# SwiGLU with seven products of quarters for eight, and the sums of weights made by adding transfers

## The chip, the cores and the metric

The kernel runs on one core of one Trainium2 chip. The metric is the device time of one execution in microseconds (us). All weights lie in HBM as float32 and are read once in the kernel before.

## The reference

A trunk of two layers over 256 tokens of 1024 features. Each layer is a SwiGLU, a mixer (attention) and a second SwiGLU, so there are four SwiGLU blocks, and only these are changed:

```python
D_MODEL, SEQ, DEPTH, D_FF = 1024, 256, 2, 2816

def rms_norm(x, g):
    y = x * lax.rsqrt(jnp.mean(x * x, axis=-1, keepdims=True) + EPS)
    return y * g

def swiglu(h, w_gate, w_up, w_down):
    return (jax.nn.silu(h @ w_gate) * (h @ w_up)) @ w_down

for layer in range(DEPTH):
    x = x + 0.5 * swiglu(rms_norm(x, ffn1_norm[layer]), *ffn1[layer])
    x = x + mixer(rms_norm(x, mix_norm[layer]))      # even or odd
    x = x + 0.5 * swiglu(rms_norm(x, ffn2_norm[layer]), *ffn2[layer])
return rms_norm(x, final_norm)
```

`w_gate` and `w_up` are 1024 x 2816, `w_down` is 2816 x 1024.

## The kernel before

**Matmuls of split numbers.** Every factor of a large product is split into a high part and a low part (`high_part`, a ScalarE copy that rounds to float32r, L319; `low_part`, a VectorE subtraction, L322). A product is three matmuls: high by high (L311), high by low (L312), low by high (L313), all in `mm`. A *piece* is one 128-row slice of weights, 512 or 384 columns wide; splitting a piece is one ScalarE and one VectorE instruction. The activations stand still (128 x 128 tiles, loaded with LDWEIGHTS) and the weights stream past them. The 256 tokens are two tiles of 128 (`tt`), so each split piece of a SwiGLU is used twice, in six matmuls.

**A SwiGLU block** (`ffn`). Gate and up go through the columns in chunks, `FF_CHUNKS = [512, 512, 512, 512, 384, 384]`. For each chunk the eight row slices of the gate are multiplied for both token tiles into PSUM tiles `s`, then those of up into `pj`. `silu` (L500, ScalarE) and `glu` (L505, VectorE) follow, then `split_T` turns the result with four TensorE transposes (L394) and splits it. The RMS factor `rstd` of a token is applied there, in `silu` and `glu`; only the gain is in the turned and split input `hT` (`prepare`, L366 to L356). The down product then runs over 22 row slices into four banks, tags `o`, `pj`, `s`, `s`. PSUM has eight banks: two `pj`, three `s`, one `o`, two `tp`.

**What sets the order.** The order on TensorE, ScalarE, VectorE and SyncE is the order in which the program emits; GpSimd's is planned by the framework. Work beside the matmuls is written as generators. `tick` runs once after each three matmuls: it steps them, and adds `rate` (0.53 pieces) to a budget from which `supply` splits the next piece, while fewer than `AHEAD = 14` split pieces wait. So the splits run up to 14 pieces ahead of the matmuls. `plan` lists the units of weights (four row slices, 1 MiB at 512 columns) in the order of their use; `load` fetches one when the first piece of the unit before is split, by one transfer from SyncE's queue (L268) into one of three `raw` buffers.

Of the kernel before, what the change touches and what calls it, by code (L numbers as in the profile page):

```python
# [1 line left out]

# [14 lines left out]
P = 128  # L17
# [22 lines left out]
X_WAIT = 5  # L40
R_WAIT = 3
GLU_WAIT = 5
NAT_WAIT = 2
ROPE_WAIT = 3
# [22 lines left out]


class Piece:


    def __init__(self, raw, uses, first):
        self.raw, self.uses, self.first, self.parts = raw, uses, first, None

# [48 lines left out]
class Trunk:  # L123
# [4 lines left out]
    def __init__(self, ctx, tc, a, out):  # L128
        self.ctx, self.tc, self.nc, self.a, self.out = ctx, tc, tc.nc, a, out
        pool = lambda name, bufs, **kw: ctx.enter_context(tc.tile_pool(name=name, bufs=bufs, **kw))  # L130
        self.one = pool("one", 1)
        self.ph = None
        self.raw = pool("raw", 3)
        self.wp = pool("wp", PIECES)
# [6 lines left out]
        self.units, self.whole, self.queue, self.live, self.due, self.half = self.plan(), [], [], 0, 0, None  # L141

    def name(self, s):
# [43 lines left out]
    def tick(self, supply=True):  # L187
        self.low()
        for task in list(self.tasks):
            task[0] -= 1  # L190
            if task[0] <= 0 and task[1] is not None:
                self.step(task)
        if supply:
            self.due += self.rate
            if self.due >= 1 and self.live < AHEAD:
                self.due = min(self.due - 1, 1)
                self.supply()


    def plan(self):  # L200


        a = self.a

        def columns(w2d, spans, units=None):
            w = sum(n for _, n in spans)
            k = 0
            for nk in units or (4, 4):
                pieces, o = [], 0
                for c0, n in spans:  # L210
                    src = w2d[k * P : (k + nk) * P, c0 : c0 + n].rearrange("(k p) n -> p k n", p=P)
                    pieces.append(((slice(0, P), slice(0, nk), slice(o, o + n)), src))
                    o += n
                yield pieces, nk, w, [2]
                k += nk

        def ffn(n, l, stage):
            c0 = 0
            for w in FF_CHUNKS:
                first = FIRST if stage == 0 and c0 == 0 else None  # L220
                yield from columns(a[n + "_w_gate"][l], [(c0, w)], first)
                yield from columns(a[n + "_w_up"][l], [(c0, w)])
                c0 += w
            for f in range(0, FF // P, 2):
                src = a[n + "_w_down"][l][f * P : (f + 2) * P, :].rearrange("(k p) n -> p k n", p=P)
                yield [(slice(0, P), src)], 2, D, [2, 3 if stage == 5 else 2]

        def even():
            w_in, w_out = a["even_w_in"][0], a["even_w_out"][0]
            for spans in ([(512, 256), (1280, 256)], [(768, 512)], [(0, 512)]):  # L230
                yield from columns(w_in, spans)
            for g in (1, 0):
                for nh in range(2):
                    pieces = []
                    for s in range(2):
                        r0 = g * 512 + s * 256
                        src = w_out[r0 : r0 + 256, nh * 512 : nh * 512 + 512].rearrange("(j p) n -> p j n", p=HD)
                        pieces.append((slice(64 * s, 64 * s + 64), src))
                    yield pieces, 4, 512, [2]

        def odd():
            w_qkv, w_out = a["odd_w_qkv"][0], a["odd_w_out"][0]
            for g in range(2):
                for i in (1, 0, 2):
                    yield from columns(w_qkv, [(i * D + g * 512, 512)])
            for g in range(2):
                for nh in range(2):
                    src = w_out[g * 512 : g * 512 + 512, nh * 512 : nh * 512 + 512].rearrange("(j p) n -> p j n", p=P)
                    yield [(slice(0, P), src)], 4, 512, [2]

# [7 lines left out]
    def load(self):  # L258
        unit = next(self.units, None)
        if unit is None:  # L260
            return
        pieces, nk, w, uses = unit
        if nk * w > 512:
            raw = self.raw.tile([P, nk, w], F32, tag="raw", name=self.name("raw"))
        else:
            raw = self.t([P, nk, w], "raw", 2)
        for sl, src in pieces:
            self.nc.sync.dma_start(raw[sl], src)  # L268
        new = [
            Piece(raw[:, k, c : min(c + 512, w)], uses[c // 512], k + c == 0) for k in range(nk) for c in range(0, w, 512)  # L270
        ]
        self.whole += new
        self.queue += new

    def supply(self):

        self.low()
        if not self.whole:
            return
        piece = self.whole.pop(0)  # L280
        if piece.first:
            self.load()
        w = piece.raw.shape[-1]
        hi = self.wp.tile([P, w], F32R, tag="hi", name=self.name("hi"))
        lo = self.wp.tile([P, w], F32R, tag="lo", name=self.name("lo"))
        self.high_part(hi, piece.raw)
        piece.parts = (hi, lo)
        self.half = piece
        self.live += 1

    def low(self):

        if self.half is not None:
            self.low_part(self.half.parts[1], self.half.raw, self.half.parts[0])
            self.half = None

# [6 lines left out]

    def mm(self, ps, lh, piece, first, last, sl=slice(None)):
        while piece.parts is None:
            self.supply()
        if piece is self.half:
            self.low()
        (h, l), (wh, wl) = lh, (t[:, sl] for t in piece.parts)
        mm = self.nc.tensor.matmul  # L310
        mm(ps, h, wh, start=first, stop=False)  # L311
# [33 lines left out]

    def part_h(self, tb, tt, i, k, j):

        hi = self.one.tile([P, P], F32R, tag=f"hT{tt}{k}h", name=self.name("th"))
        lo = self.one.tile([P, P], F32R, tag=f"hT{tt}{k}l", name=self.name("tl"))
        gain = self.gains[:, i * KD + k : i * KD + k + 1]  # L350
# [9 lines left out]
    def prepare(self, tt, i, half, dest):  # L360
# [6 lines left out]
        yield 1  # L367
        his = [self.part_h(tb, tt, i, half * 4 + j, j) for j in range(4)]
        yield 1
# [65 lines left out]
    def project(self, hT, pieces, tag):  # L435
        ps = self.bank(tag)
        n = len(pieces)
        for k in range(n):
            self.mm(ps[:, : pieces[k].raw.shape[-1]], hT[k], pieces[k], k == 0, k == n - 1)
        return ps  # L440
# [12 lines left out]
    def first_gates(self, W):  # L453
# [5 lines left out]
        def turn(j):  # L459
# [6 lines left out]
            return banks  # L466

        def parts(j, banks):
            for tt in range(NT):
                now.hT[tt] += [self.part_h(banks[tt], tt, 0, 2 * j + i, i) for i in range(2)]  # L470
            for i in range(2):
# [11 lines left out]
        for j in range(KD // 2):  # L483
# [3 lines left out]
            for k in (2 * j, 2 * j + 1):  # L487
                for tt in range(NT):
                    self.mm(ps[tt], now.hT[tt][k], W[k], k == 0, k == KD - 1)
        return ps  # L490

    def ffn(self):
        nc = self.nc
        self.rate = RATE
        gT = [[], []]
        tasks = [[], []]

        def silu(tt, w, g, s):
            yield 1
            nc.scalar.activation(s[:, :w], g[:, :w], AF.Silu, scale=self.rstd_of(tt))  # L500

        def glu(tt, ci, w, u, s):
            yield 1
            m = self.t([P, 512], "glu", 2)
            nc.vector.scalar_tensor_tensor(m[:, :w], u[:, :w], self.now.r[tt], s[:, :w], op0=ALU.mult, op1=ALU.mult)  # L505
            yield GLU_WAIT
            yield from self.split_T(m, w // P, f"g{tt}_{ci}_", gT[tt])

        for ci, w in enumerate(FF_CHUNKS):
            G = self.take(KD)  # L510
            S = []
            if self.now.n + ci == 0:
                both = self.first_gates(G)
            for tt in range(NT):
                g = both[tt] if self.now.n + ci == 0 else self.project(self.ready(tt), G, "s")
                S.append(self.t([P, 512], "silu", 2))
                self.start(silu(tt, w, g, S[tt]))
            U = self.take(KD)
            for tt in range(NT):
                u = self.project(self.now.hT[tt], U, "pj")  # L520
                tasks[tt].append(self.start(glu(tt, ci, w, u, S[tt])))
        nf = FF // P
# [3 lines left out]
        if self.next.n == 6:  # L526
            self.last_gain = self.t([P, D], "last_gain")
            self.last = [self.t([P, D], f"last{tt}") for tt in range(NT)]
            self.nc.sync.dma_start(self.last_gain, self.a["final_norm"].partition_broadcast(P))
# [3 lines left out]
        def use(f, tt, i):  # L533
            while len(gT[tt]) <= f:
                self.tick(False)
# [396 lines left out]
    def after(self, tt, sl, nxt):  # L932
# [9 lines left out]
        x, w, done = self.x[tt][:, sl], sl.stop - sl.start, sl.stop == D  # L942
        sq = self.t([P, 512], "sq", 2)
        v = self.two.tile([P, 1], F32, tag="last_v", name=self.name("v"), bufs=4)
# [59 lines left out]
    def run(self):  # L1004
# [20 lines left out]

        self.next = Stage(0)

# [29 lines left out]
_INS = [  # L1057
    "x", "ffn1_w_gate", "ffn1_w_up", "ffn1_w_down", "ffn2_w_gate", "ffn2_w_up", "ffn2_w_down",
    "even_w_in", "a_q_norm", "a_k_norm", "b_sink", "even_w_out",
# [25 lines left out]
```

## Time and profile before

| | |
|---|---|
| three runs | 979.34 us median (979.08 to 980.24) |
| profiled execution | 978.92 us, span 977.1 us |
| TensorE matmul busy | 965.5 us, 99% of the span, 4908 matmuls |
| VectorE busy | 607.7 us, 62% |
| ScalarE busy | 546.0 us, 56% |
| GpSimd busy | 85.7 us, 9% |
| SyncE's DMA queue | 170.23 MB, 54.0% of what 16 DMA engines could be busy |

The profile is of one execution. A row of the groups gives line, engine, operation, output and inputs, shapes and count, then busy time, mean nanoseconds of one, and the idle time of the engine ahead of these instructions with what ended it. The matmul rows of a timeline overlap, since one matmul starts before the last one has left the array: the pitch from start to start is what one costs, not its listed length.

### The profile page before, as it was taken

To read this page: it belongs to the slowest core of one execution; us is meant where nothing else is said; L and a number is where in the kernel's file an instruction comes from. 1 tells how busy PE (TensorE), PEld (TensorE's weight loads), DVE (VectorE), ACT (ScalarE), POOL (GpSimd) and SP (SyncE) were. 2 spreads that over 40 slices of the span, in tenths; PEclk is the share of its full clock that TensorE was granted. 3 is DMA by queue.
4 is the path that set the end of the run, shared out by engine and by line. 5 is a ranking of instruction groups with operands and counts; after the bars stand their busy time and mean duration, and the time that the engine had idled before them with its cause. 6 is when DMAs were issued, how large, how long until landed. Compare 5 with 4: busy or idle time off the path is not lost.

```text
span 977.1 us, 13724 instructions
## 1 busy us (share of the span) xinstructions
PE 965.5 (99%) x4908; PEld 818.6 (84%) x4908; DVE 607.7 (62%) x1195; ACT 546.0 (56%) x1152; POOL 85.7 (9%) x152
## 2 busy tenths in 40 slices
PE   9999999999999999999999999999999999999997
PEld 6888998877788889988888899888888888889886
DVE  6565575488866555654655566548879675555643
ACT  7544564477786544544644446447777664545430
POOL 0020000063420000000000000101331000000002
PEclk9999999999999999999999999999999999999999
DMA  8665576554226555766456456646545355547621
GB/s 290 223 205 172 182 251 214 168 135 120 96 91 208 176 157 158 246 215 197 148 176 197 145 173 231 223 153 197 181 128 170 130 172 181 186 131 235 237 87 43
DMA packets 82373, 171.70 MB, mean 176 GB/s; under 512 B 3712, under 2 KB 25216, under 8 KB 82304
## 3 DMA queue, kind: packets, MB, share of 16 engines
q1 hardware_dynamic: 81728, 170.23, 54.0%
q8 instruction: 38, 0.62, 0.3%
q10 hardware_dynamic: 576, 0.59, 0.2%
q14 instruction: 31, 0.25, 0.1%
HBM read 169.76 MB, written 1.05 MB: 175 GB/s over the span
## 4 chain that ended last, share of the span: by engine, by line
PE 95%; DVE 2%; ACT 1%; POOL 1%; issue 1%; DMA 0%; POOLq 0%; ACTq 0%
PE pj L311 14%; PE pj L313 14%; PE pj L312 14%; PE s L313 13%; PE s L312 13%; PE s L311 13%; PE tp L394 2%; PE o L311 2%; PE o L312 2%; PE o L313 2%; PE o L609 2%; PE tp L688 1%; PE tp L366 1%; PE s L624 1%; PE s L625 1%; DVE lo L322 1%
## 5 line engine op out<-in xcount | busy, mean ns | idle before, releaser
L322 DVE TENSOR_TENSOR lo<-raw,hi 128x512 fp32r<-128x512 f32 (+1 forms) x664 | 423.2, 671 | 239.1 <-ACT hi L319 235.0
L319 ACT ACTIVATE hi<-raw 128x512 fp32r<-128x512 f32 (+1 forms) x664 | 371.9, 606 | 169.4 <-PE s L313 102.4
L311 PE MATMUL pj<-hi,th 128*128 128x512 f32 (+1 forms) x512 | 197.8, 386 | 0.0
L313 PE MATMUL pj<-hi,tl 128*128 128x512 f32 (+1 forms) x512 | 192.8, 377 | 0.0
L312 PE MATMUL pj<-lo,th 128*128 128x512 f32 (+1 forms) x512 | 192.5, 376 | 0.0
L311 PE MATMUL s<-hi,th 128*128 128x512 f32 (+1 forms) x400 | 152.1, 380 | 0.0
L313 PE MATMUL s<-hi,tl 128*128 128x512 f32 (+1 forms) x400 | 149.2, 373 | 0.0
L312 PE MATMUL s<-lo,th 128*128 128x512 f32 (+1 forms) x400 | 148.9, 372 | 0.0
L313 PEld LDWEIGHTS pj<-hi,tl 128*128 128x128 f32 x512 | 96.1, 188 | 15.5
L311 PEld LDWEIGHTS pj<-hi,th 128*128 128x128 f32 x512 | 96.4, 188 | 13.0 <-issue 0.3
L312 PEld LDWEIGHTS pj<-lo,th 128*128 128x128 f32 x512 | 96.4, 188 | 12.8
L319 ACT ACTIVATE g_h<-tp 128x512 fp32r<-128x512 f32 (+1 forms) x48 | 27.0, 563 | 126.4 <-PE tp L394 126.4
L313 PEld LDWEIGHTS s<-hi,tl 128*128 128x128 f32 x400 | 75.2, 188 | 11.2
L312 PEld LDWEIGHTS s<-lo,th 128*128 128x128 f32 x400 | 75.3, 188 | 10.5 <-DVE lo L322 0.2
L311 PEld LDWEIGHTS s<-hi,th 128*128 128x128 f32 x400 | 75.3, 188 | 10.1
L313 PE MATMUL s<-hi,g_l 128*128 128x512 f32 (+2 forms) x198 | 73.6, 372 | 0.0
L312 PE MATMUL s<-lo,g_h 128*128 128x512 f32 (+2 forms) x198 | 73.5, 371 | 0.0
L311 PE MATMUL s<-hi,g_h 128*128 128x512 f32 (+2 forms) x198 | 73.5, 371 | 0.0
L505 DVE SCALAR_TENSOR_TENSOR glu<-pj,rstd,silu 128x512 f32<-128x512 f32 (+1 forms) x48 | 33.7, 702 | 45.1 <-PE pj L313 45.1
L500 ACT ACTIVATE silu<-s,rstd 128x512 f32<-128x512 f32 (+1 forms) x48 | 31.4, 654 | 51.1 <-PE s L313 50.6
L331 POOL TENSOR_TENSOR rstd<-var,mhalf 128x1 f32<-128x1 f32 (+2 forms) x16 | 12.9, 808 | 375.8 <-DVE var L329 375.8
L322 DVE TENSOR_TENSOR g_l<-tp,g_h 128x512 fp32r<-128x512 f32 (+1 forms) x48 | 30.8, 642 | 23.1 <-ACT g_h L319 23.1
(245 smaller groups left out, 1133.7 us busy)
## 6 DMA issues: line engine op xcount, KB each, us to landing
raw<-in_ffn_w_down SPq DMA_DIRECT2D x44, 1024.0 KB, 5.0
raw<-in_ffn_w_up SPq DMA_DIRECT2D x32, 1024.0 KB, 5.2
raw<-in_ffn_w_gate SPq DMA_DIRECT2D x30, 1024.0 KB, 5.1
raw<-in_ffn_w_gate SPq DMA_DIRECT2D x16, 768.0 KB, 4.4
raw<-in_ffn_w_up SPq DMA_DIRECT2D x16, 768.0 KB, 4.4
raw<-in_odd_w_qkv SPq DMA_DIRECT2D x12, 1024.0 KB, 5.2
raw<-in_even_w_in SPq DMA_DIRECT2D x4, 1024.0 KB, 5.1
raw<-in_even_w_out SPq DMA_DIRECT2D x8, 512.0 KB, 5.7
```

What stands on the lines that cost most here:

```text
L311: mm(ps, h, wh, start=first, stop=False)
L312: mm(ps, h, wl, start=False, stop=False)
L313: mm(ps, l, wh, start=False, stop=last)
L319: self.nc.scalar.activation(hi, src, AF.Copy)
L322: self.nc.vector.tensor_tensor(lo, src, hi.bitcast(F32), op=ALU.subtract)
L331: nc.gpsimd.tensor_tensor(r[:, :n], v[:, :n], self.mhalf[:, :n], op=ALU.pow)
L366: nc.tensor.transpose(tb[:, j * P : (j + 1) * P], self.x[tt][:, b * P : (b + 1) * P], self.ident)
L394: self.nc.tensor.transpose(tb[:, i * P : (i + 1) * P], src[:, i * P : (i + 1) * P], self.ident)
L500: nc.scalar.activation(s[:, :w], g[:, :w], AF.Silu, scale=self.rstd_of(tt))
L505: nc.vector.scalar_tensor_tensor(m[:, :w], u[:, :w], self.now.r[tt], s[:, :w], op0=ALU.mult, op1=ALU.mult)
L609: self.nc.tensor.matmul(O[64 * s : 64 * s + 64, i * P : i * P + P], v(b0 + i, s, kc), pT[s][:, i, kc, :], start=(kc == 0), stop=(kc == 1),)
L624: nc.tensor.matmul(S[:, i, :], q, kz[s], start=True, stop=False)
```

## The change

`FF_CHUNKS` becomes `[("plain", 384), ("pair", 1024), ("plain", 384), ("pair", 1024)]`. A plain chunk is computed as before. A pair takes 1024 columns of gate and of up at once. The input (256 x 1024) is cut into quarters of 128 tokens by 512 features, and the 1024 x 1024 weights into quarters of 512 x 512. The four quarter products of the output are made with seven products of sums of quarters (Strassen's algorithm in Winograd's form) in place of eight.

- *Sums of weights.* A pair's unit is one quarter (1 MiB). Quarter tiles `X0`, `X1` (gate, up) are loaded, split, and then have another quarter added three times, `Y` tiles once, by transfers issued from GpSimd's queue with `accum_op=ALU.add`, two of 512 KB for each sum. The order is X, Z, X+, Y, X+, Y+, X+, each for gate and then up: of 14 MiB a pair, 6 are plain loads and 8 are adding transfers. An addition is issued when the last low part of the old content is made (`Split.then`).
- *Splits.* In a SwiGLU block, one instruction splits two pieces (128 x 2 x 512); the mixers and the first gate keep single ones (`narrow`). A weight sum is used by one product only.
- *Input quarters.* `normalised` multiplies the input by `rstd` and gain on VectorE, turns it (16 transposes a block), splits it, and keeps whole copies; `sums` makes the four sums of input quarters from these, once a block.
- *Products.* `pair` accumulates seven products each for gate and up in three banks each (`s`, `s`, `s`; `pj`, `pj`, `o`). Some banks are copied out to SBUF (`keep`) and accumulated further; `result` adds or subtracts such a copy and applies silu and product.

```diff
-FF_CHUNKS = [512, 512, 512, 512, 384, 384]
-PIECES = 15
+FF_CHUNKS = [("plain", 384), ("pair", 1024), ("plain", 384), ("pair", 1024)]
+SPLITS = 7
 AHEAD = 14
+MORE = {"X": 3, "Y": 1}
+PLAIN_RATE = 0.62
+PAIR_RATE = 1.0
...
+        def pair(both, c0):
+            ...
+            yield from load("X", 0, 0)
+            yield from load("Z", 1, 0)
+            yield from add("X", 0, 1)
+            yield from load("Y", 1, 1)
+            yield from add("X", 1, 1)
+            yield from add("Y", 0, 1)
+            yield from add("X", 1, 0)
...
+    def again(self, key, srcs):
+        splits = []
+        olds, more = self.held.pop(key)
+        for old, src in zip(olds, srcs):
+            add = lambda raw=old.raw, src=src: self.nc.gpsimd.dma_start(raw, src, accum_op=ALU.add)
+            if old.ended:
+                add()
+            else:
+                old.then = add
+            splits.append(Split(old.raw, False, False))
...
+        self.low_part(lo[:, sl], split.raw[:, sl], hi[:, sl])
+        if sl.stop == split.raw.shape[1]:
+            split.ended = True
+            if split.then is not None:
+                split.then()
...
+    def normalised(self, A, F):
+        ...
+                nc.vector.scalar_tensor_tensor(
+                    xn, self.x[tt][:, sl], self.now.r[tt], gain[:, sl], op0=ALU.mult, op1=ALU.mult
+                )
+                yield A_WAITS[0]
+                tb = self.turned(xn)
+                ...
+                self.high_part(flat(hi), tb)
+                nc.scalar.activation(whole, tb, AF.Copy)
+                yield A_WAITS[2]
+                self.low_part(flat(lo), tb, flat(hi))
...
+    def pair(self, A, S, f0, gT):
+        tags = (("s", "s", "s"), ("pj", "pj", "o"))
+        ...
+            for k in range(4):
+                self.mm(X[i][x], quarter[k], W[k], first and k == 0, k == 3, on=not first)
+        ...
+        steps = [
+            (0, a(0, 0), True, (0, 0), None),
+            (1, a(0, 1), True, None, (0, 0, "X + kept")),
+            (2, s(0), True, (1, 1), None),
+            (2, s(1), False, None, None),
+            (0, s(2), False, (0, 1), None),
+            (0, s(3), False, None, (1, 1, "kept - X")),
+            (0, a(1, 1), False, None, (1, 0, None)),
+        ]
+        for n, step in enumerate(steps):
+            for i in range(2):
+                behind(i, *step)
+                if n == 4:
+                    self.start(late(i))
```

A step names the accumulator, the input quarter, whether the accumulator starts anew, what is kept and what is given out. The framework's memory for descriptors of transfers issued from GpSimd is doubled (`dynamic_dma_scratch_size` 1024 to 2048).

More of the change, by code (lines that the diff above doesn't have):

```diff
@@ L1 @@
 from contextlib import ExitStack
+from functools import partial
 import numpy as np
@@ L66, with __init__, step @@
 }
+class Split:
+    def __init__(self, raw, first, narrow):
+        self.raw, self.first, self.narrow = raw, first, narrow
+        self.parts, self.made, self.ended, self.then = None, 0, False, None
+    def step(self):
+        return 1 if self.narrow else self.raw.shape[1]
 class Piece:
-    def __init__(self, raw, uses, first):
-        self.raw, self.uses, self.first, self.parts = raw, uses, first, None
+    def __init__(self, split, i, uses):
+        self.split, self.i, self.uses, self.w = split, i, uses, split.raw.shape[-1]
 def constants():
@@ L258, in load @@
     def load(self):
[L259 to L263, printed above, removed]
+        self.owed += 1
+        while self.owed:
+            unit = self.put_back or next(self.units, None)
+            self.put_back = None
+            if unit is None:
+                return
+            if len(unit) == 2:
+                self.again(*unit)
+                continue
+            if unit[0].startswith("X") and self.planned > self.now.n:
+                self.put_back = unit
+                return
+            self.load_unit(*unit)
+            self.owed -= not unit[0].startswith("X")
@@ L272, in load, with coming @@
-        self.whole += new
-        self.queue += new
+        if w == D:
+            views = [raw[:, k, :].rearrange("p (a w) -> p a w", a=2) for k in range(nk)]
+        else:
+            views = [raw[:, k : min(k + 2, nk), :] for k in range(0, nk, 2)]
+        splits = [Split(view, n == 0 and not key.startswith("X"), narrow) for n, view in enumerate(views)]
+        if key and key[0] in MORE:
+            self.held[key] = [splits, MORE[key[0]]]
+        self.coming(splits, uses)
+    def coming(self, splits, uses):
+        self.whole += splits
+        for split in splits:
+            self.queue += [Piece(split, i, uses[i % len(uses)]) for i in range(split.raw.shape[1])]
@@ L302, in take, with mm @@
         return got
-    def mm(self, ps, lh, piece, first, last, sl=slice(None)):
-        while piece.parts is None:
+    def mm(self, ps, lh, piece, first, last, sl=slice(None), on=False):
+        split = piece.split
+        while split.made <= piece.i:
             self.supply()
-        if piece is self.half:
+        if self.half is not None and self.half[0] is split and self.half[1].start <= piece.i:
             self.low()
-        (h, l), (wh, wl) = lh, (t[:, sl] for t in piece.parts)
-        mm = self.nc.tensor.matmul
+        (h, l), (wh, wl) = lh, (t[:, piece.i, sl] for t in split.parts)
+        mm = partial(self.nc.tensor.matmul, skip_group_check=on)
         mm(ps, h, wh, start=first, stop=False)
@@ L367, in prepare @@
         yield 1
-        his = [self.part_h(tb, tt, i, half * 4 + j, j) for j in range(4)]
+        tiles = self.quarter(tt, half)
+        his = [self.part_h(tb, tt, i, half * 4 + j, j, tiles) for j in range(4)]
         yield 1
@@ new lines, in sums, with parts @@
+    def sums(self, S, F):
+        nc = self.nc
+        def parts(whole, tt, half):
+            hi, lo = self.quarter(tt, half)
+            flat = lambda t: t.rearrange("p a b -> p (a b)")
+            self.high_part(flat(hi), whole)
+            yield 1
+            self.low_part(flat(lo), whole, flat(hi))
+            S.append([(hi[:, i, :], lo[:, i, :]) for i in range(4)])
+        add = lambda o, a, b, op: nc.vector.tensor_tensor(o, a, b, op=op)
+        a11, a12, a21, a22 = (F[q] for q in ((0, 0), (0, 1), (1, 0), (1, 1)))
+        add(a22, a21, a22, ALU.subtract)
+        yield from parts(a22, 0, 0)
+        yield 1
+        add(a21, a11, a21, ALU.subtract)
+        add(a11, a22, a11, ALU.subtract)
+        yield 1
+        add(a12, a11, a12, ALU.add)
+        yield from parts(a12, 0, 1)
+        yield 1
+        yield from parts(a11, 1, 0)
+        yield 1
+        yield from parts(a21, 1, 1)
@@ L492, in ffn, with silu @@
     def ffn(self):
         nc = self.nc
[L494 to L498, printed above, removed]
+        gT = [{}, {}]
+        A, F, S = {}, {}, []
+        self.spawn(self.normalised(A, F), NORM_WAIT)
+        def silu(tt, w, g, s, raw):
             yield 1
-            nc.scalar.activation(s[:, :w], g[:, :w], AF.Silu, scale=self.rstd_of(tt))
-        def glu(tt, ci, w, u, s):
+            nc.scalar.activation(s[:, :w], g[:, :w], AF.Silu, scale=self.rstd_of(tt) if raw else 1.0)
@@ new lines, in ffn @@
+        f0 = 0
+        for ci, (kind, w) in enumerate(FF_CHUNKS):
+            if kind == "pair":
+                self.rate = PAIR_RATE
+                if not S:
+                    while len(F) < 4:
+                        self.tick(False)
+                    self.start(self.sums(S, F))
+                self.pair(A, S, f0, gT)
+                f0 += w // P
+                continue
+            self.rate = PLAIN_RATE
+            raw = ci == 0
+            lhs = lambda tt: self.ready(tt) if raw else A[tt, 0] + A[tt, 1]
```

213 lines of the change are left out of this document (158 added, 55 removed).

## The prediction

> **What bounds the kernel now.** The page comes first: engines, DMA queues, the chain that ended last.
>
> ```profile
> span 977.1 us, 13724 instructions
> PE 965.5 (99%) x4908; PEld 818.6 (84%) x4908; DVE 607.7 (62%) x1195; ACT 546.0 (56%) x1152; POOL 85.7 (9%) x152
> q1 hardware_dynamic: 81728, 170.23, 54.0%
> PE 95%; DVE 2%; ACT 1%; POOL 1%; issue 1%; DMA 0%; POOLq 0%; ACTq 0%
> raw<-in_ffn_w_gate SPq DMA_DIRECT2D x30, 1024.0 KB, 5.1
> ```
>
> TensorE is busy for 99% of the span and carries 95% of the chain; nothing else has more than 2%. The matrix work is the time. VectorE (62%), ScalarE (56%) and DMA (54%) have room on average. A table by stretch says whether that holds in the third SwiGLU block (columns: busy of PE, weight load, DVE, ACT, POOL; clock; DMA share; GB/s):
>
> ```profile
> 478.00:664.00 186.00, 186.00 (x895) 159.75 (x895) 106.79 (x187) 95.56 (x185) 4.90 (x6) 1.00 0.57 187
> ```
>
> It does: TensorE never rests in 186 us, at full clock, while VectorE is busy for 57% and DMA for 57%. So a matmul left out saves its full pitch, as long as the other three keep up. The pitch stands in the timeline of TensorE: 30 matmuls of 512 columns lie between the first two rows below, 24 of 384 between the next two. The last row, from the chain, is a group of four transposes.
>
> ```profile
> 90.00 0.39 PE L311 MATMUL pj<-hi,th 128*128 128x512 f32 x1
> ...
> 96.80 0.39 PE L311 MATMUL pj<-hi,th 128*128 128x512 f32 x1
> 575.80 0.33 PE L312 MATMUL pj<-lo,th 128*128 128x384 f32 x1
> ...
> 579.97 0.33 PE L312 MATMUL pj<-lo,th 128*128 128x384 f32 x1
> 472.73 0.44 PE tp L366 x4
> ```
>
> 6.80 / 30 is 0.2267 us for 512 columns, 4.17 / 24 is 0.174 us for 384, 0.44 / 4 is 0.11 us for a transpose.
>
> **TensorE's part of the change.** Gate and up of one block are now 4 chunks x 2 x 8 slices x 2 token tiles x 3 = 384 matmuls of 512 and 192 of 384. A pair is 7 products x 2 x 4 slices x 3 = 168 of 512, so two pairs are 336; the plain chunks are the same 192. That is 48 fewer, 48 x 0.2267 = 10.9 us. `normalised` adds 16 transposes, 1.8 us. Net 9.1 us a block: gate and up, with their 44 transposes (4.8 us), go from 87.1 + 33.4 + 4.8 = 125.3 to 76.2 + 33.4 + 4.8 + 1.8 = 116.2. For four blocks 36.5 us, the most that this change can save. One place loses some of it. Down's second bank is the `pj` that the pair's last product filled, so it waits for one tick and the VectorE product `u*g` (0.75 us below), perhaps behind a split, with only three matmuls of the `o` bank (0.68 us) in front: 0 to 2 us, taken as 1.2 a block. Down itself, the mixers and the tail stay.
>
> **VectorE and ScalarE.** Each weight sum is split and used once: a pair has 56 pieces (before: 32 for the same columns), in 28 instructions of double width. Runs back to back and the other instructions concerned:
>
> ```profile
> 482.30 3.10 DVE L322 TENSOR_TENSOR lo<-raw,hi 128x512 fp32r<-128x512 f32 x5 [0.15 <-ACT hi L319]
> 89.77 1.49 DVE L322 TENSOR_TENSOR lo<-raw,hi 128x384 fp32r<-128x384 f32 x3
> 481.64 2.73 ACT L319 ACTIVATE hi<-raw 128x512 fp32r<-128x512 f32 x5
> 89.57 2.17 ACT L319 ACTIVATE hi<-raw 128x384 fp32r<-128x384 f32 x5
> L446 DVE SCALAR_TENSOR_TENSOR x<-pj,x 128x512 f32<-128x512 f32 x20 | 13.7, 686 | 11.8 <-PE pj L313 11.7
> L505 DVE SCALAR_TENSOR_TENSOR glu<-pj,rstd,silu 128x512 f32<-128x512 f32 x32 | 23.9, 747 | 35.2 <-PE pj L313 35.2
> L322 DVE TENSOR_TENSOR g_l<-tp,g_h 128x512 fp32r<-128x512 f32 x32 | 22.0, 686 | 18.3 <-ACT g_h L319 18.3
> L500 ACT ACTIVATE silu<-s,rstd 128x512 f32<-128x512 f32 x32 | 22.0, 690 | 37.0 <-PE s L313 36.6 <-ACT hi L319 0.3
> L319 ACT ACTIVATE g_h<-tp 128x512 fp32r<-128x512 f32 x32 | 19.2, 599 | 94.1 <-PE tp L394 94.1
> ```
>
> VectorE takes 0.62 us for 512 columns and 0.50 for 384, 0.12 per 128 more; 1024 columns come to 1.11 us by the same step. A pair: 28 x 1.11 = 31.1, and 6 additions, 4 products and 4 low parts of results at 0.69, 9.7: 40.8 us, against 38.1 of matmuls. The first pair has `sums` beside it, eight at 0.62: 45.8. A plain chunk has eight splits of 768 columns (0.86 each), two products and two low parts: 9.2, the first one 15.0 with `normalised` (4 x 0.75 + 4 x 0.69). Together 110.8 us against TensorE's 116.2. VectorE is the bound inside pairs, and its cover is the lead: 14 split pieces are 14 x 3 x 0.2267 = 9.5 us of matmuls, more than the first pair's deficit of 7.7, and the second plain chunk (16.7 + transposes against 9.2) gives it back. Down has 44 pieces as 22 instructions, 25 us in 60, so a lag at the second pair's end is absorbed there. At 95% of TensorE's time some waits in queue order will show through; between 0 (all covered) and 10.4 (both deficits paid in full), 2.5 us a block, near the covered end because the lead exceeds each deficit. ScalarE has 28 x 0.99 = 27.8 for the splits, plus 6 copies and 4 high parts at 0.60 and 4 silus at 0.69: 36.6 of 38.1 in a pair: it fits under VectorE and adds nothing unless a copy queues behind a split that waits for data.
>
> **The adding transfers.** Each pair moves 14 MiB, 8 by adding. No transfer of before adds or comes from GpSimd's queue. What is near:
>
> ```profile
> 486.00:488.00 2.00, 2.00 (x10) 1.65 (x9) 0.24 (x1) 1.48 (x3) 0.00 (x0) 1.00 1.01 393
> 496.00:498.00 2.00, 2.00 (x12) 1.69 (x11) 0.43 (x1) 1.58 (x4) 0.00 (x0) 1.00 1.03 398
> L268 SPq DMA_DIRECT2D raw<-in_ffn_w_gate x51: 367/368/568, 1.2 to 873.3; - x51
> SPq L268 <- DVE lo L322: 761.2, 153, 12.7
> L856 POOL TENSOR_TENSOR bias<-rows,mats 128x384 f32<-128x384 f32 x16 | 19.1, 1231 | 6.6 <-DMA rows<-in_c_rel_bias 6.6
> ```
>
> When all engines work, copies of these weights run at 393 GB/s: 2.7 us per MiB. Let an added MiB cost *a*. Low end 2.7 (only the write counts, which is a copy's), high end 5.4 (it reads two operands, like two copies one after the other). Work until the last addition of a block lands, given that three loads wait in `raw` already: 0.75 + 6 + 3 + 6 = 15.75 MiB of loads, 42.5 us, and 16 a; then 5 us of idle DMA (one landing, 5.1) and 4 us for splitting and multiplying the last two sums: 51.5 + 16 a. It stays under 116.2 up to a = 4.0, and passes the 125.3 of before at a = 4.6. I take the middle, 4.05, as no row is nearer to one end: the sum is 116.3, just hidden, by buffers that fill and drain; with such a tie some splits are late, and I put 1.5 us a block on it. The Trainium skill, "Collectives: The Full Stack", section "The bandwidth ceiling: the fold count and why AG ≠ RS ≠ AR", says that an adding transfer halves the rate because its two reads share one ring (62.28 against 32.35 GB/s over two engines); as an estimate, its 16.2 GB/s per engine would make a 4.05 and the sum as taken, its ratio of 1.93 against the copies here 5.2 and a block slower than before. No row of before shows which.
>
> The chain split, add, split also has to turn: from the end of one split of X0 to the next lie three other products, 8.2 us, and the lead on top. A landing of 5.1 us plus issue leaves some 3. What is queued behind a late addition: the ScalarE high part of that sum waits at the head of its queue, behind it the copies `keep` and silus, behind those TensorE's next use of the bank. Additions leave SyncE's queue, where most time is spent waiting for free buffers (761.2 us on `lo`, the row above); the pair's first loads of X wait there for the old X's last split, and Z and Y queue behind them, an arrival some 17 us (a plain chunk) ahead of use. GpSimd issues 16 additions a pair, one per 2.4 us.
>
> **Sum.** Per block −9.1 + 1.2 + 2.5 + 1.5 = −3.9; times four −15.6. Narrow splits in the mixers, the smaller first transfers and the gain's load lie under TensorE's 99% and are put at nothing; without cover a load of 512 KB costs its landing, some 5 us once. The profiled execution took 978.92 us (1.8 over its span, 0.4 under the median of 979.34): 978.9 − 15.6 = 963.
>
> **Rivals.**
> *Additions nearly free* (a near 2.7, waits covered): −9.1 + 1.2 a block, 978.9 − 31.6 = 947. For it: 43% of DMA time is idle in the block. Against: VectorE's 95%.
> *DMA becomes the bound, slower.* At a = 5.4 the block's gate and up end at 51.5 + 86.4 = 137.9 against 125.3: +12.6, four times 50, so 1029. It decides from a = 4.6 on. For it: two operands are read for each write. Its place: ScalarE waiting for DMA inside pairs. This is what the ratio in the Trainium skill's page named above would do.
> *GpSimd cannot issue fast enough.* SyncE's issue takes 0.37 us, GpSimd's slower work 1.23 (rows above). From (38.1 + 9.5) / 16 = 3.0 us per addition on it sets the pace; at 3.5 a pair grows by 56 − 47.6 = 8.4 us, eight pairs 67, less the 15.6 saved: 1030.
> *VectorE in full.* Both deficits paid, 10.4 a block in place of 2.5: 963 + 32 = 995.
> *No change:* the sums cancel, a near 4.5: 979.
>
> **Chances.** What measurement tells from no change here is about 0.2%, 2 us. The forecast (950 to 975) 0.46; additions nearly free (940 to 950) 0.17; DMA the bound 0.18, GpSimd's issue 0.08 and VectorE in full 0.07, all slower; no change 0.04. The forecast's own case is faster throughout. Faster 0.63, same 0.04, slower 0.33. The range goes from 942 (36.5 saved in full) to 1029 (a = 5.4), which leaves out the issue rival's worse half and a few of each end; the likeliest case alone is 950 to 975.
>
> **What would show it.** Matmuls: 4908 − 192 + 64 = 4780. A second DMA queue with 128 transfers of 512 KB, 67 MB, shows *a*: its packet time against the bytes. Double splits of 1.11 us on VectorE; VectorE near 95% of TensorE's in the blocks; a wait of the first `pj` in down. Were ScalarE's `hi` to wait for DMA by more than 10 us a block, the middle for *a* was too low; were GpSimd's issues to take over 3 us each, the issue rival holds; TensorE idle on VectorE's `lo` without a DMA behind it would be the VectorE case. The prediction is wrong on the slower side if TensorE's share of the span falls below 95%.

## The result, and the profile after

The changed kernel takes 1168.87 us (median of four runs, 1163.87 to 1172.57) against 979.55: 1.193 times the time before, 95% interval 1.188 to 1.197. The forecast was 963, and the upper end of its range 1029.

The page of the changed kernel, engines, granted clock, DMA by slices, queues and adding transfers:

```profile
span 1167.2 us, 13494 instructions
PE 1010.0 (87%) x4780; PEld 822.2 (70%) x4780; DVE 762.7 (65%) x1127; ACT 657.7 (56%) x1068; POOL 244.9 (21%) x284
PEclk9988988999999889889998797999999998798899
DMA  8887996546157979965669799554544579799540
q1 hardware_dynamic: 73280, 153.45, 39.6%
q0 software_dynamic: 35392, 69.21, 33.0%
X<-in_ffn_w_gate POOLq DMA_DIRECT2D x48, 512.0 KB, 8.6
X<-in_ffn_w_up POOLq DMA_DIRECT2D x48, 512.0 KB, 9.6
```

TensorE has 4780 matmuls, as worked out, and is idle for 13% of the span. A packet of the adding queue q0 takes 0.330 x 1167.2 x 16 / 35392 = 174 ns of an engine, one of SyncE's q1 by the same working 101, at 2.0 and 2.1 KB on average. Both queues carry some packets of other sizes; those of exactly 2 KB take 184 and 97 ns in the trace. The clock falls below full in the slices of the SwiGLU blocks. Before, a slice at less than 9 tenths did not occur.

Where the time went can be read between landmarks of TensorE's timeline. "Gate and up" runs from the last matmul of the work before to the first of down. The table has sums over the four blocks of the profiled execution, in us; its last column is the median of the runs:

| | gate and up | two mixers | run |
|---|---|---|---|
| before | 510.7 | 209.6 | 979.6 |
| after | 690.9 | 219.0 | 1168.9 |
| e1_copy | 578.1 | 219.1 | 1052.8 |
| e2_none | 565.5 | 218.1 | 1045.3 |
| e3_half | 577.8 | 219.0 | 1053.4 |
| e4_plain | 545.0 | 218.6 | 1024.0 |
| e5_onepair | 623.3 | 218.9 | 1099.3 |
| e7_none_waits | 557.6 | 218.9 | 1035.2 |
| e8_none_nolow | 496.6 | 218.7 | 973.9 |
| e9_plain_raw | 515.1 | 218.8 | 992.6 |
| e10_adds_nolow | 650.2 | 218.3 | 1126.8 |
| e11_none_halflow | 530.5 | 218.7 | 1011.0 |
| e12_plain_late | 526.6 | 218.7 | 1004.0 |
| e13_half_waits | 519.6 | 218.4 | 1002.1 |
| e14_plain_single | 511.9 | 211.2 | 982.0 |

Down takes 61.4 to 61.5 us a block before and after (65.4 in the last). So 180 of the 189 us lie in gate and up, 9 in the mixers. The third block's gate and up lasts 167.6 us in the kernel after, from 573.1 to 740.6. A window that nearly covers it (columns as in the prediction's window row):

```profile
571.00:738.00 167.00, 134.09 (x591) 110.14 (x590) 116.75 (x142) 101.19 (x143) 43.80 (x37) 0.89 0.87 203
```

167 us with VectorE busy for 117 and DMA for 87%. This one row does not say which of the two it is. The waits of the kernel after name both (who waits <- for whom: us in total, times, longest):

```profile
ACT hi L422 <- DMA X<-in_ffn_w_up: 51.9, 27, 3.3
ACT hi L422 <- DMA X<-in_ffn_w_gate: 40.7, 23, 4.3
PE tp L501 <- DVE u L699: 30.6, 12, 4.9
PE s L414 <- ACT g L680: 28.4, 8, 6.2
PE pj L414 <- ACT u L680: 26.4, 7, 4.8
```

ScalarE's high parts wait for the `X` tiles for 93 us in total, about 23 a block: this is the sign that the prediction gave for too low an *a* (over 10 us a block). The copies `keep` (L680) stand behind them in ScalarE's queue, and TensorE waits 55 us for these copies, in the order that the prediction described. The 31 us at `u` (L699) are waits for VectorE.

### The profile page after: what moved, and what is told of

Its sections match the earlier page's. It is cut to its first block, busy times and chain, and to the rows that moved or that the text cites. A ratio compares the mean times of both kernels' runs of the same rounds, so it can differ in the third digit from the quotient of the medians.

```text
span 1167.2 us, 13494 instructions
## 1 busy us (share of the span) xinstructions
PE 1010.0 (87%) x4780; PEld 822.2 (70%) x4780; DVE 762.7 (65%) x1127; ACT 657.7 (56%) x1068; POOL 244.9 (21%) x284
## 3 DMA queue, kind: packets, MB, share of 16 engines
q1 hardware_dynamic: 73280, 153.45, 39.6%
q0 software_dynamic: 35392, 69.21, 33.0%
## 5 line engine op out<-in xcount | busy, mean ns | idle before, releaser
L425 DVE TENSOR_TENSOR lo<-raw,hi 128x1024 fp32r<-128x1024 f32 (+3 forms) x354 | 356.9, 1022 | 209.1 <-ACT hi L422 208.2
L422 ACT ACTIVATE hi<-raw 128x1024 fp32r<-128x1024 f32 (+3 forms) x354 | 307.1, 886 | 214.4 <-PE s L416 142.7
L425 DVE TENSOR_TENSOR lo<-X,hi 128x1024 fp32r<-128x1024 f32 (+1 forms) x130 | 156.9, 1217 | 113.1 <-ACT hi L422 111.6
L422 ACT ACTIVATE hi<-X 128x1024 fp32r<-128x1024 f32 (+1 forms) x130 | 134.6, 1049 | 108.7 <-DMA X<-in_ffn_w_up 51.9
L414 PE MATMUL pj<-hi,th 128*128 128x512 f32 (+1 forms) x256 | 108.0, 422 | 26.6 <-ACT u L680 26.4
L414 PE MATMUL s<-hi,th 128*128 128x512 f32 (+1 forms) x208 | 88.1, 424 | 30.0 <-ACT g L680 28.4
L415 PE MATMUL pj<-lo,th 128*128 128x512 f32 (+1 forms) x256 | 102.3, 400 | 2.3 <-DVE lo L425 2.3
L416 PE MATMUL pj<-hi,tl 128*128 128x512 f32 (+1 forms) x256 | 101.6, 397 | 0.8 <-DVE tl L462 0.8
L415 PE MATMUL s<-lo,th 128*128 128x512 f32 (+1 forms) x208 | 85.6, 412 | 2.5 <-DVE lo L425 2.5
L416 PE MATMUL s<-hi,tl 128*128 128x512 f32 (+1 forms) x208 | 84.4, 406 | 1.1 <-DVE tl L462 1.1
## 6 DMA issues: line engine op xcount, KB each, us to landing
raw<-in_ffn_w_down SPq DMA_DIRECT2D x44, 1024.0 KB, 5.3
raw<-in_ffn_w_gate SPq DMA_DIRECT2D x16, 1024.0 KB, 5.9
raw<-in_ffn_w_up SPq DMA_DIRECT2D x16, 1024.0 KB, 7.6
raw<-in_odd_w_qkv SPq DMA_DIRECT2D x12, 1024.0 KB, 5.1
```

Source lines behind the costliest of these rows:

```text
L415: mm(ps, h, wl, start=False, stop=False)
L416: mm(ps, l, wh, start=False, stop=last)
L422: self.nc.scalar.activation(hi, src, AF.Copy)
L425: self.nc.vector.tensor_tensor(lo, src, hi.bitcast(F32), op=ALU.subtract)
```

## The experiments

**Transfers alone, and the sums replaced.** m1_transfers is a kernel of transfers only. The next three change what an addition transfers; all else stays:

```diff
-add = lambda raw=old.raw, src=src: self.nc.gpsimd.dma_start(raw, src, accum_op=ALU.add)
+add = lambda raw=old.raw, src=src: self.nc.gpsimd.dma_start(raw, src)                    # e1_copy
+add = lambda: None                                                                       # e2_none
+add = lambda raw=old.raw, src=src: self.nc.gpsimd.dma_start(raw[:, 0:1, :], src[:, 0:1, :], accum_op=ALU.add)   # e3_half
```

m1_transfers. 

> Transfers alone, with nothing beside them, five stretches over four 1 MiB buffers: 24 copies of 512 KB from SyncE's queue, 24 from GpSimd's, 24 adding ones with rows of 2 KB, 24 adding ones with rows of 4 KB, and 6 adding ones one at a time. RATE: copies 2.7 to 3 us per MiB from both queues, adding ones 5.4 to 5.9. CHAIN or ISSUE: adding ones under 4 us per MiB as long as several are under way, and one alone 6 us or more. If GpSimd's issue set the pace, its copies would take as long as its adding transfers.

The page of m1_transfers: DMA and rate by slices of 5.7 us; then windows inside three of its five stretches, the copies from SyncE, the copies from GpSimd and the additions with rows of 4 KB (columns: busy of DVE and POOL, clock, DMA share, GB/s):

```profile
DMA  6999999999999999999999999999999995555554
GB/s 222 390 387 387 387 389 387 389 387 387 386 340 206 205 207 200 206 204 206 203 205 203 212 211 210 213 210 213 209 212 210 211 206 79 82 84 88 91 91 183
L39 POOL DMA_DIRECT2D b<-in_ffn_w_up x24 | 28.8, 1199 | 34.7 <-issue 34.7
```

```profile
3.00:25.00 22.00, 0.00 (x0) 0.00 (x0) 1.00 1.05 389
30.00:60.00 30.00, 0.00 (x0) 15.35 (x22) 1.00 1.03 388
128.00:172.00 44.00, 0.00 (x0) 16.54 (x20) 1.00 1.07 211
```

Copies run at 387 to 390 GB/s, from SyncE's queue and from GpSimd's alike. Adding transfers run at 205 GB/s with rows of 2 KB and 211 with 4 KB, at full DMA share: 1 MiB takes 2.7 us copied and 5.1 us added, a little under the 5.4 to 5.9 expected. GpSimd needs 1.2 us for an issue and then idles; it is not the limit. RATE it is, even with nothing beside it. The ratio of 1.90 agrees with the 1.93 between all-gather and reduce-scatter in the Trainium skill, "Collectives: The Full Stack", section "The bandwidth ceiling: the fold count and why AG ≠ RS ≠ AR". The 16.2 GB/s per engine that the prediction worked out from it does not carry over: 205 / 16 is 12.8.

e1_copy. 

> The 128 adding transfers become plain copies of the same bytes, issued from the same queue at the same places (the sums are left out: each copy overwrites). Theory RATE (an added MiB occupies the DMA engines for 5.4 us or more, twice a copy's 2.7): the DMA work of a block's gate and up falls from about 140 to about 90 us, under TensorE's 116, so most of the 190 us of loss goes: 950 to 985. Theory CHAIN (the round trip split, issue, landing, split of 9 us sets the pace, whatever the bytes): a copy lands some 3 us earlier, a third of the loss goes: about 1100. Theory ISSUE (GpSimd's 1.2 us per issue and its descriptors set the pace): nothing changes, 1150 to 1170.

e2_none. 

> No transfer for the sums at all: the same tile is split again (the sums are left out). All splits, products and results stay. RATE, CHAIN and ISSUE alike: what is left is TensorE's work with VectorE's cover, 947 to 963 by the sum of the prediction. If VectorE's 95% were a second cause of the loss: 995 or more.

e3_half. 

> Each adding transfer adds one of its two 128-row slices (half the sums are left out): half the bytes, the same number of issues, the same chains. RATE: adding falls from 94 to 47 us a block, DMA work to about 93 us, under TensorE's 116: 955 to 1000. CHAIN: a landing is perhaps 2 us earlier, 1110 to 1140. ISSUE: 1150 to 1170.

e1_copy took 1052.76 us (ratio to before 1.074, 1.072 to 1.076), e2_none 1045.28 (1.067, 1.065 to 1.068), e3_half 1053.4 (1.075, 1.073 to 1.077). Halving the bytes of the additions does the same as making copies of them: both cost about 8 us over no transfer at all, where the full additions cost 124. ISSUE and CHAIN would have kept most of that. The fall of 116 us is RATE's. But none came near what was expected (950 to 985 for e1_copy, 947 to 963 for e2_none): without any transfer for sums the kernel is still 65 us slower than before. There was a second cause, in which DMA has no part.

**The second cause.** Four kernels: e4_plain and e5_onepair change the chunks of the changed kernel, e7_none_waits and e8_none_nolow are built on e2_none:

```diff
-FF_CHUNKS = [("plain", 384), ("pair", 1024), ("plain", 384), ("pair", 1024)]
+FF_CHUNKS = [("plain", 384), ("plain", 512), ("plain", 512), ("plain", 384), ("plain", 512), ("plain", 512)]   # e4_plain
+FF_CHUNKS = [("plain", 384), ("plain", 512), ("pair", 1024), ("plain", 512), ("plain", 384)]                   # e5_onepair
...
-A_WAITS = [2, 1, 1, 1]
-GLU_WAIT = 5
+A_WAITS = [4, 1, 1, 1]      # e7_none_waits, on e2_none
+GLU_WAIT = 12
...
         hi, lo = split.parts                       # e8_none_nolow, on e2_none: lo is hi for a pair's pieces
-        self.low_part(lo[:, sl], split.raw[:, sl], hi[:, sl])
+        if lo is not hi:
+            self.low_part(lo[:, sl], split.raw[:, sl], hi[:, sl])
```

e4_plain. 

> The changed kernel with plain chunks alone (384, 512, 512, 384, 512, 512), so no pair, no sum and no adding transfer; the turned and normalised input and the splits of double width stay. The second cause of the loss (65 us without any sum's transfer) is either in the pairs or in the rest. Theory PAIRS (VectorE's results in a pair come late, TensorE stands in order at their transposes): here 979.5 plus 4 x 1.8 for the 64 transposes, 983 to 992. Theory REST (normalising and double splits delay each block's start): 1000 or more.

e5_onepair. 

> One pair a block in place of two: plain 384, plain 512, pair 1024, plain 512, plain 384. Half the sums, half the adding transfers. RATE with the second cause in the pairs: half of each loss, 979.5 + (190 / 2) = 1060 to 1080; if the free DMA time of the plain chunks around one pair took up a part of it, 1010 to 1050. Under 979 only if the pair's density alone were the trouble.

e7_none_waits. 

> As e2_none (no transfer for sums, the sums left out), and TensorE's transposes of results are emitted 12 ticks behind VectorE's product in place of 5 (GLU_WAIT), those of the normalised input 4 in place of 2 (A_WAITS). Theory QUEUE (TensorE, which goes in order, stands at transposes of results that VectorE, late by a few us, has not made; the lead of 14 pieces covers weights alone): 1045 falls to 985 to 1015. Theory LOAD (VectorE's total work in a pair is the bound): 1035 to 1050.

e8_none_nolow. 

> As e2_none, and no low part is made of a pair's weight pieces (the high part stands in for it in the matmuls, whose number stays), which takes 28 of VectorE's 1.22 us instructions out of each pair. QUEUE and LOAD alike: VectorE is never late, 945 to 965. If TensorE's stalls have another source (a bank that is not free, ScalarE): 1000 or more.

e8_none_nolow took 973.87 us, 0.994 of before (0.993 to 0.995): with VectorE relieved and no sums' transfers, the smaller number of matmuls does pay, though 9 us short of the 945 to 965 expected. Against e2_none the low parts of the pairs' weights cost 71 us. e4_plain took 1024.03 (1.045, 1.043 to 1.047) without a pair in it, so two more causes had to be looked for, not one: the rest of the change alone costs 44 us. e5_onepair took 1099.33 (1.122, 1.120 to 1.124), more than the 1060 to 1080 expected: 75 us over e4_plain for one pair a block, where the changed kernel has 145 for two. A pair costs 18 to 19 us wherever it stands, and the free DMA time of the chunks around a lone pair did not help. e7_none_waits took 1035.24 (1.056, 1.054 to 1.058), 10 us less than e2_none; it falls into LOAD's range, and QUEUE as put there explains only those 10 us.

e2_none, what TensorE waited for (releaser, us in total, times, longest), then its longest wait in the third block and VectorE's work ahead of it:

```profile
PE tp L501 <- DVE u L699: 19.1, 11, 4.9
PE tp L501 <- DVE u L613: 15.2, 10, 2.1
PE s L414 <- DVE g L693: 8.2, 8, 1.1
PE pj L415 <- DVE lo L425: 3.3, 6, 0.8
```

```profile
554.38 1.08 PE L501 MATMUL tp<-mats,u 128*128 128x128 f32 x4 [4.92 <-DVE u L699]
```

```profile
551.82 0.68 DVE L693 TENSOR_TENSOR u<-pj,u 128x512 f32<-128x512 f32 x1
552.42 1.22 DVE L425 TENSOR_TENSOR lo<-raw,hi 128x1024 fp32r<-128x1024 f32 x1
553.55 0.69 DVE L699 TENSOR_TENSOR u<-u,g 128x512 f32<-128x512 f32 x1
```

TensorE hardly waits for weights (`lo`, 3.3 us into `pj` and 7.4 in all). It stands at the transposes of results: `u` at L699 in a pair, L613 in the normalised input at the block's start. VectorE works through its queue in order, a split between the two steps of the result, and TensorE goes in order too. ScalarE waits for VectorE as well: its silu waits for VectorE's step with the kept bank (L693, L697 after the edit of e11_none_halflow), and the next high parts queue behind the silu. The rows of e2_none and of e11_none_halflow (below), which makes half of the low parts of the pairs' weights:

```profile
ACT g L696 <- DVE g L693: 47.0, 24, 2.7
```

```profile
ACT g L700 <- DVE g L697: 23.8, 16, 1.9
```

What part of the loss goes this way was not tested.

**Each of the three causes alone: the block's start, the additions, VectorE in the pairs.**

```diff
-        self.spawn(self.normalised(A, F), NORM_WAIT)
-            raw = ci == 0
+            raw = True               # e9_plain_raw, on e4_plain
...
-A_WAITS = [2, 1, 1, 1]
-            raw = ci == 0
+A_WAITS = [6, 1, 1, 1]               # e12_plain_late, on e4_plain
+            raw = ci <= 1
...
+            split.two = uses != [1]                   # e10_adds_nolow: e8's edit on the changed kernel
+            split.two = uses != [1] or n % 2 == 0     # e11_none_halflow, on e2_none
```

e9_plain_raw. 

> As e4_plain (plain chunks alone), and the normalised input is not made either: all chunks use hT as before, with rstd applied behind. What is left of the change are the splits of double width, the tiles of four slices and the lead in units of two pieces. Theory NORM (making the normalised input at a block's start stalls TensorE): gate and up return to 126 us a block; with the 9 us that the mixers lost, 986 to 992. Theory WIDE (double-width splits delay the first pieces): 1010 to 1024.

e12_plain_late. 

> As e4_plain, with the transposes of the normalised input emitted 6 ticks behind VectorE's product in place of 2 (A_WAITS), and the second chunk on hT so that there is time for it. QUEUE at the block's start (TensorE stands at these four groups of transposes until VectorE gets to the products): 1024 falls to 995 to 1008. If the stall is VectorE's and ScalarE's load there: 1018 to 1026.

e9_plain_raw took 992.57 us (1.013, 1.012 to 1.015) and its gate and up 515.1, near the 510.7 of before: of e4_plain's 44 us, 31 belong to the normalised input. The 64 transposes account for 7. e12_plain_late took 1004.0 (1.025, 1.024 to 1.026): placing the transposes later, with the second chunk on `hT` to make room, wins 20 of these 31. At the block's start QUEUE holds. TensorE's waits in e4_plain and in e12_plain_late, where the row of `u` at L613 is gone:

```profile
PE tp L501 <- DVE u L613: 16.5, 10, 2.1
PE tp L472 <- DVE x L553: 1.7, 3, 1.3
```

```profile
PE tp L472 <- DVE x L553: 1.7, 3, 1.3
PE tp L1027 <- POOL kra L980: 1.7, 1, 1.7
```

e10_adds_nolow. 

> The changed kernel with its adding transfers, and no low part of a pair's weight pieces (the high part stands in for it), so VectorE is never late. If the adding transfers cost what DMA's rate alone makes them: gate and up at 45 us of loads, 94 of sums and about 9 of gaps, 149 a block against 120 in e8_none_nolow, 974 plus 4 x 29 = 1090. If part of the 124 us was the chain split, add, split made longer by a late VectorE: 1040 to 1070.

e10_adds_nolow took 1126.75 us (1.150, 1.148 to 1.152), over both expectations. The first row is a window of the third block's gate and up, without its first 12 us; for comparison the block in e8_none_nolow, the same without the additions:

```profile
567.00:712.00 145.00, 119.35 (x531) 98.78 (x530) 42.01 (x59) 88.22 (x112) 40.46 (x35) 0.89 0.95 223
```

```profile
473.00:593.00 120.00, 118.09 (x591) 101.82 (x590) 51.95 (x86) 99.57 (x143) 5.05 (x5) 1.00 0.42 143
```

VectorE is busy for 42 of 145 us, DMA for 95%: here DMA is the bound. Over the whole block DMA is busy for 93% of 157.1 us; the chain split, add, split can account for no more than the other 11 us. The additions cost 153 us with VectorE relieved and 124 with VectorE late, so the costs overlap: VectorE adds 71 us when DMA is free and 42 (1168.9 − 1126.8) when DMA is the bound.

e11_none_halflow. 

> As e2_none, and the low part is made for every second double split of a pair only: VectorE's work in a pair falls from about 42 to 26 us, well under TensorE's 38. Theory LOAD (the loss is VectorE's excess over TensorE's time): all of it goes, 974 to 982. If each VectorE instruction in the pair cost time, whatever the sum: half way, 1005 to 1015.

e13_half_waits. 

> As e11_none_halflow (no transfer for sums, half of the low parts of a pair's weights), with TensorE's transposes of results 12 ticks behind VectorE's product in place of 5 and those of the normalised input 4 in place of 2. With all low parts this edit saved 10 of 1045. Theory QUEUE FIRST (where VectorE is not overloaded, what is lost is TensorE standing at transposes placed too close behind VectorE's work): 1011 falls to 980 to 990. Theory EACH (every VectorE instruction of a pair costs its share wherever the transposes stand): 1003 to 1011.

e11_none_halflow took 1010.99 us (1.032, 1.030 to 1.034): half of the low parts, half of the loss. LOAD, by which only VectorE's excess over TensorE's time costs, is refuted. e13_half_waits took 1002.09 (1.023, 1.021 to 1.024), 9 us less: just under EACH's 1003 and far from QUEUE FIRST's 990. TensorE's waits in e11_none_halflow, then in e13_half_waits:

```profile
PE tp L505 <- DVE u L617: 15.0, 10, 2.1
PE tp L505 <- DVE u L703: 12.7, 9, 3.0
```

```profile
PE tp L505 <- DVE u L617: 7.5, 7, 1.5
PE s L418 <- ACT g L684: 6.8, 3, 2.3
PE s L418 <- DVE g L697: 6.7, 6, 1.1
```

With the transposes moved, the wait for `u` at L703 (L699 before the edit) goes, and new ones stand at matmuls into `s`, for ScalarE's copy `keep` and VectorE's `result`. Some of these banks are read and then accumulated further by the next product of the same matrix, one product of 2.7 us later. Moving one consumer exposes the next nearest.

e14_plain_single. 

> As e9_plain_raw (plain chunks, input not normalised), and the splits are single again, with 14 buffers of one piece in place of 7 of two. It tells what the 13 us are that e9_plain_raw still loses, 9 of them in the mixers. If the buffers held in twos shorten the lead: 980 to 984. If it is the input held in tiles of four slices, whose first matmul waits for all four: 990 to 993.

Its edit makes each view of a `Split` one piece and `SPLITS` 14. It took 981.96 us (1.0023, 1.0014 to 1.0033), 10.6 less than e9_plain_raw; the mixers fall from 218.8 to 211.2. There the splits are single in both kernels, so these 7.6 us are the buffers held in twos. The 1.6 us that the mixers keep were not pursued.

No kernel here beats the one before with its whole computation. A repair would need sums of weights at less than the price of these transfers, the low parts off VectorE and the results further from their use, together worth at most the prediction's 36.5 us.

## Why the prediction was wrong, by its own steps

- *TensorE's part.* The count was right: 4780 matmuls. The gain is there in e8_none_nolow, whose gate and up are 14 us under before, where −9.1 + 1.2 a block makes 32. Of the 18 us missing, 10 are in the first block and 2.5 in each of the others; TensorE's waits for `u` of `normalised` (L617) come to 7.8 of them.
- *The adding transfers: the step that failed first.* The middle between 2.7 and 5.4 us per MiB was taken "as no row is nearer to one end". Measured alone it is 5.1. Beside the other transfers 33.0% x 1167.2 us over the 66 MiB of q0 (64 of them added, 2 of the gain) is 5.8: past the high end. The formula was right in kind: 51.5 + 16 x 5.8 is 144 us a block, over its own break-even of a = 4.6; e10_adds_nolow has 157 to 158, the kernel after 165 to 170 in blocks two to four. Two smaller terms make most of the rest. By the same working a load costs 39.6% x 1167.2 us over 146 MiB, 3.2 us per MiB and not 2.7, which adds 7 us over 15.75 MiB. And where the formula has 9 us without transfers at the end, DMA is idle for 11 us of the third block in e10_adds_nolow and for 12% of 167.6 us, 20 us, in the kernel after. The rival "DMA becomes the bound" was this mechanism, with too low a price: 50 us over the kernel before, where e10_adds_nolow, with VectorE out of the way, has 147. Unknown and decisive, *a* should have been the first number, not one term of four: with a uniform chance between its own ends the slower case, from 4.6 to 5.4, had (5.4 − 4.6) / 2.7 = 0.30, more than the 0.18 given.
- *VectorE.* Its durations were near (1.14 us back to back for 1.11) and the work too: 115.5 us busy in a block of e2_none for 110.8. What failed is the cover, "its cover is the lead: 14 split pieces are 14 x 3 x 0.2267 = 9.5 us of matmuls". The lead covers weights. Results, transposes and banks have only 5 and 4 ticks, 2.7 to 3.4 us, and TensorE stops at the first of them that is late. Taken at 2.5 us a block, it cost 17 (69 / 4) without DMA in the way. "VectorE in full" (10.4) was too small too.
- *The block's start.* `normalised` was priced by its transposes, 1.8 us. VectorE's four products on the way, with transposes two ticks behind them, cost another 6 (31 − 7 over four blocks), a wait that the text did not name though it named the queue for `keep`.
- *Put at nothing:* the narrow splits in the mixers, "under TensorE's 99%". The mixers lost 9 us; the buffers in twos are 7.6 of them, and the rest was not pursued.
- *GpSimd's issue*, a rival at 0.08, is not the bound: 1.2 us each, under the 3 us that it would have needed, and idle between.

How much the lower clock adds was not separated. It was no step of the sum. The busy time of the same 4780 matmuls bounds it: 941.5 us in e8_none_nolow, 964.2 in e2_none and 1010.0 in the kernel after. So at most 23 of the 71 us between the first two, and at most 69 of the kernel's 189, are matmuls that ran longer.

## What to carry to other kernels

When one resource has no row in the profile and the bounds of its price straddle break-even, measure it by itself before the rest is added up; an adding transfer took 1.9 times as long here as a copy of the same bytes, so bytes were not the measure of its cost. A lead of split weights covers weights only: the cover of an engine that falls behind is the shortest distance, in program order, between any result of it and the in-order engine that uses it, PSUM banks included. With all, half and none of the low parts (1045, 1011 and 974 us) the loss went in proportion to VectorE's work, and not only where that work exceeds TensorE's time.

## What the runs showed of the hardware that was not expected

Waits of a few us halve TensorE's clock for a while. From the timeline of TensorE in the kernel after (128 x 512 each):

```profile
143.68 0.49 PE L414 MATMUL o<-hi,th 128*128 128x512 f32 x1 [1.64 <-ACT hi L422]
144.93 0.50 PE L415 MATMUL o<-lo,th 128*128 128x512 f32 x1 [0.76 <-DVE lo L425]
145.27 0.39 PE L416 MATMUL o<-hi,tl 128*128 128x512 f32 x1
148.83 1.09 PE L501 MATMUL tp<-mats,u 128*128 128x128 f32 x4 [3.16 <-DVE u L699]
...
151.00 0.63 PE L414 MATMUL s<-hi,th 128*128 128x512 f32 x1
151.42 0.63 PE L415 MATMUL s<-lo,th 128*128 128x512 f32 x1
151.85 0.63 PE L416 MATMUL s<-hi,tl 128*128 128x512 f32 x1
152.28 0.63 PE L414 MATMUL s<-hi,th 128*128 128x512 f32 x1
...
153.24 0.40 PE L414 MATMUL s<-hi,th 128*128 128x512 f32 x1
153.48 0.39 PE L415 MATMUL s<-lo,th 128*128 128x512 f32 x1
```

After the wait of 3.16 us the pitch is 0.43 us, and some 4 us later 0.23 again. The same stretch in windows of 3.4 us (columns as in the prediction's window row, the clock third from the end):

```profile
142.60:146.00 3.40, 1.23 (x3) 0.48 (x3) 2.10 (x2) 3.40 (x5) 1.20 (x1) 1.00 1.10 255
146.00:149.40 3.40, 0.57 (x3) 0.60 (x4) 3.40 (x5) 3.36 (x5) 1.20 (x1) 0.50 1.14 205
149.40:152.80 3.40, 3.40 (x11) 2.72 (x10) 3.29 (x4) 2.16 (x4) 1.72 (x2) 0.50 1.10 180
152.90:156.30 3.40, 3.40 (x17) 2.79 (x16) 2.91 (x3) 1.89 (x2) 1.79 (x2) 1.00 1.11 199
```

The clock fell at 146.0 us, when the wait of 3.16 us had hardly begun: in the 3.4 us ahead, TensorE had been busy for only 1.23 us, with waits of 1.64 and 0.76 us. It came back behind a window full of matmuls. Shorter waits alone seldom do this: e4_plain has ten of up to 2.1 us at the blocks' starts and a mean clock of 0.997. The mean granted clock is 0.935 in the kernel after, 0.985 in e2_none and 0.996 in e8_none_nolow, against 0.998 before. The Trainium skill, "TensorE: Matmul & The Clock Gate", Part 1, has the array drop to half rate after an idle window of about 3.4 us and need as long a busy one to return. The trace agrees with the length, since the 6.8 us at half rate are two such windows; but the window ahead of the drop was not idle here, it held 1.23 us of matmuls. So a stall costs more than its length, though where DMA is the bound the slow matmuls may lie under the next wait.
